# A gathered cumulative sum and projection: eight of 128 stores cut into 120 and 8 partitions

## The chip, the core and the metric

The kernel runs on one core of a Trainium2 chip. The metric is the device time of one launch, in microseconds; lower is better. Times before are the median of three runs. A profile of one execution is read beside them; its engines are PE (TensorE matmul), PEld (TensorE weight load), DVE (VectorE), ACT (ScalarE), POOL (GpSimd) and SP (SyncE).

## The reference

```python
B, S, N, D = (16, 4096, 2048, 512)
x        # (B, S, D) float32
indices  # (B, N) int64: for each batch, N different rows of S, sorted
w        # (D, D) float32

b_idx = np.arange(B)[:, None]
gathered = x[b_idx, indices, :].copy()
cs = np.cumsum(gathered, axis=1)
return np.matmul(cs, w).astype(np.float32)
```

For each of 16 batches, 2048 rows of 512 numbers are gathered, summed cumulatively along the rows, and multiplied by a 512 x 512 matrix. 67 MB are gathered and 67 MB stored.

## The kernel before

The 16 x 2048 rows are cut into T = 256 tiles of 128 rows, NT = 16 to a batch. Two tiles (R = 2) make a pair; G = 128 pairs. Each engine runs its own list of instructions, written out by hand at build time, and waits on semaphores; nothing is scheduled by a planner. `Lane.need` emits a wait only where that engine has not waited for as much before.

For each tile t the steps are:

- `gather(t)` (line 126, GpSimd): an indirect DMA brings 128 rows of x, one to a partition, into one half of a pair's buffer `g32` (8 buffers, 16 tiles). It waits until the cast of the tile 16 earlier has freed the buffer. GpSimd issues the gathers back to back, in order.
- `cast(t, n)` (line 141, ScalarE): to float16, one tile or a whole pair at once (n = 2), after the gathers of these tiles have landed. The casts run ahead of the drains by `far` tiles: 2 at the start, rising by one every 8 tiles to FAR = 10, and falling again by one every 6 tiles towards the end.
- `sums(t)` (line 152, TensorE): four matmuls against a triangular matrix give the cumulative sums within the tile, transposed. `carry(t)` (lines 171 and 184, VectorE) adds the last column of the tile before and writes float16 into `cst`.
- `project(u)` (line 195, TensorE): four matmuls by w into a PSUM bank `pb` (4 of them). TensorE's order interleaves sums and projections, with the sums up to LEAD = 4 tiles ahead, fewer at both ends.
- `drain(u)` (line 207, ScalarE): copies the PSUM bank into one half of the pair's output buffer `ob` (NO = 8 buffers of 128 partitions x 2 x 512 float32).
- `store(g)` (lines 216 and 221, SyncE): when both halves are drained, one DMA of 512 KB writes the pair, each partition holding two neighbouring rows of the output, 4 KB in a run. The triangular matrix `ut` of all pairs but the first and last puts the rows in this order. The first and last pair (`PLAIN`) keep the rows in order and are stored tile by tile.

ScalarE's list is, for each tile u: at the first tile of a pair, a wait until the store that last used this `ob` buffer has landed (the store of eight pairs earlier); then the casts due at u; then the drain of u.

```python
    for u in range(T):
        if u % R == 0:
            if u == R * NO:
                act.need(s_of, 16)
            act.need(s_o[u // R % NO], 16 * (u // R // NO))
        for t, n in casts[u]:
            cast(t, n)
        drain(u)
```

SyncE's list holds the loads of indices and w, then the 128 stores in order, then waits for the last stores to land. Every DMA adds 16 to its semaphore when all of it has landed.

Of the kernel before, what the change touches and what calls it, by code (L numbers as in the profile page):

```python
# [7 lines left out]
P = 128  # L8
# [19 lines left out]
def kernel(  # L28
# [7 lines left out]
    nc = tc.nc  # L36
# [3 lines left out]
    R = 2  # L40
# [4 lines left out]
    G = T // R  # L45
# [8 lines left out]
    NB = 4  # L54
    NC = 4
    NO = 8
    assert D == 512 and N % (R * P) == 0 and T % P == 0

    x_flat = x.rearrange("b s d -> (b s) d")
# [17 lines left out]
    cst = [const.tile([P, DC, R, P], FP16, name=f"cst{i}") for i in range(NC)]  # L77
    ob = [const.tile([P, R, D], FP32, name=f"ob{i}") for i in range(NO)]
    pa = [ps.tile([P, DC, R, Q], FP32, name=f"pa{i}") for i in range(NA)]
# [4 lines left out]
    def sem(name):  # L84
        return tc.alloc_semaphore(name)
# [9 lines left out]
    s_g = [sem(f"s_g{i}") for i in range(NG)]  # L95
    s_o = [sem(f"s_o{i}") for i in range(NO)]
    s_a = sem("s_a")
    s_d = sem("s_d")
    s_b = sem("s_b")
    s_e = sem("s_e")  # L100

    pool, pe, dve, act, sp = (
        Lane(e) for e in (nc.gpsimd, nc.tensor, nc.vector, nc.scalar, nc.sync)
    )
# [32 lines left out]
    def cast(t, n):  # L137
        g, r = divmod(t, R)
        for u in range(t, t + n):
            act.need(s_g[u % NG], 16 * (u // NG + 1))  # L140
        nc.scalar.copy(  # L141
            out=g16[g % NH][:, r : r + n], in_=g32[g % (NG // R)][:, r : r + n]
        ).then_inc(s_c, 1)
# [60 lines left out]
    def drain(u):  # L204
        g, j = divmod(u, R)
        act.need(s_b, u + 1)
        nc.scalar.copy(out=ob[g % NO][:, j], in_=pb[u % NB][:]).then_inc(s_e, 1)  # L207

    def store(g):
        b, h = divmod(g, GB)  # L210
        rows = out[b, h * R * P : (h + 1) * R * P, :]
        if g in PLAIN:
            for j in range(R):
                sp.need(s_e, R * g + j + 1)
                done = s_ol[j] if g else (s_o[0], s_of)[j]
                nc.sync.dma_start(
                    out=rows[j * P : (j + 1) * P, :], in_=ob[g % NO][:, j]
                ).then_inc(done, 16)
            return
        sp.need(s_e, R * (g + 1))  # L220
        nc.sync.dma_start(
            out=rows.rearrange("(p j) d -> p j d", j=R), in_=ob[g % NO][:]
        ).then_inc(s_o[g % NO], 16)


    with nc.allow_non_contiguous_dma(reason="a few indices, one per partition"):
        for k, eng in enumerate((nc.sync, nc.scalar)):
            t = k * R
            eng.dma_start(  # L229
                out=idx_first[:, t : t + R, :],  # L230
                in_=indices[0, t * P : (t + R) * P]
# [7 lines left out]
    for k in range(KI):  # L239
        nc.sync.dma_start(  # L240
            out=idx64[:, k, :], in_=idx_rows[k * P : (k + 1) * P, :]
        ).then_inc(s_idx[k], 16)
    for g in range(G):
        store(g)
    for g in range(G - NO, G - 1):
        sp.need(s_o[g % NO], 16 * (g // NO + 1))
    for j in range(R):
        sp.need(s_ol[j], 16)

# [5 lines left out]
        out=ident[:],  # L255
        in_=ident[:],
# [7 lines left out]
        out=ut[:],  # L264
        in_=ut[:],
# [9 lines left out]
        out=uq[:],  # L275
        in_=uq[:],
# [23 lines left out]
    for k in range(KI):  # L300
# [3 lines left out]
            out=pb[k % NB][:, :P], in_=idxf[:, k, :], identity=ident[:]  # L304
# [37 lines left out]
    for u in range(T):  # L342
        if u % R == 0:
            if u == R * NO:
                act.need(s_of, 16)
            act.need(s_o[u // R % NO], 16 * (u // R // NO))
        for t, n in casts[u]:
            cast(t, n)
        drain(u)
# [30 lines left out]
```

## Time and profile before

| | |
|---|---|
| Median of three runs (lowest, highest) | 351.18 us (350.65, 351.27) |
| The profiled execution: its own time | 351.18 us |
| Its span, first to last instruction | 349.5 us |
| Mean granted TensorE clock | 0.995 |
| PE busy, share of the span | 307.3 us, 88% |
| ACT busy | 264.2 us, 76% |
| POOL busy | 243.9 us, 70% |
| DVE busy | 179.0 us, 51% |
| Moved by DMA | 135.91 MB, mean 389 GB/s |
| Stores of a pair (line 221), median to landing | 126, 512.0 KB each, 7.4 us |
| Gathers (line 126), median to landing | 252, 8.4 us |

Busy time is summed over all stages of the run; it does not say which engine others wait for. The profiled time of 351.18 us is 1.7 us over the span: launch and end lie around it. In the list of DMA issues the last column is the median time from issue to landing. Instruction groups show count, busy time, mean duration in ns, and the idle time of the engine just before them with what ended most of it.

### The profile page before, as it was taken

The numbers are of one execution on the slowest core, as the hardware profiler recorded it, in microseconds if no ns is written. First come the engines' busy times: TensorE is split into PE (matmuls) and PEld (weight loads), VectorE is DVE, ScalarE is ACT, GpSimd is POOL, SyncE is SP. The second block draws the span as 40 slices with busy tenths as digits, with TensorE's granted clock in tenths as the row PEclk, the third lists the DMA queues.
The fourth block names the chain that finished last, engine by engine and source line by source line (L and its number), as shares of the span: only waits on it lengthen the run. The fifth ranks groups of instructions, "written<-read, shape, count | busy, mean of one in ns | idle before, by whom it ended". The sixth has DMA issues, their size and how long they took to land.

```text
span 349.5 us, 5668 instructions
## 1 busy us (share of the span) xinstructions
PE 307.3 (88%) x2071; PEld 153.9 (44%) x2071; DVE 179.0 (51%) x263; ACT 264.2 (76%) x408; POOL 243.9 (70%) x266
## 2 busy tenths in 40 slices
PE   5878877998898899999898989999898989988984
PEld 2334433554444444444444444444444445544431
DVE  1335554665554555555555545555554556654441
ACT  3368876886787778787787867777787788787883
POOL 6777777777777777777777777777777777777000
PEclk9899999999999999999999999999999999999999
DMA  7799999999999999999999999999999999999974
GB/s 238 218 299 366 389 397 399 400 399 399 403 413 409 412 409 412 415 414 413 413 416 416 409 414 412 411 411 415 410 413 412 410 415 412 414 415 415 416 320 186
DMA packets 40635, 135.91 MB, mean 389 GB/s; under 512 B 6816, under 2 KB 7072, under 8 KB 40608
## 3 DMA queue, kind: packets, MB, share of 16 engines
q0 software_dynamic: 20480, 67.13, 49.7%
q1 hardware_dynamic: 19568, 67.91, 48.3%
q10 hardware_dynamic: 560, 0.53, 0.4%
q8 instruction: 16, 0.26, 0.3%
q14 instruction: 11, 0.09, 0.1%
HBM read 68.42 MB, written 67.11 MB: 388 GB/s over the span
## 4 chain that ended last, share of the span: by engine, by line
POOL 34%; DMA 25%; issue 14%; PE 13%; ACT 11%; DVE 1%; SPq 0%; ACTq 0%
POOL g L126 34%; DMA g<-in_x_dram,idxg 24%; PE pb L195 8%; ACT g L141 8%; ACT ob L207 3%; PE pa L152 3%; DMA idx<-in_indices_dram 1%; PE pb L291 1%; DVE cst L184 1%; SPq L238 0%; DVE cst L171 0%; PE pb L303 0%; SPq L229 0%; ACTq L23 0%; DVE idxf L298 0%
## 5 line engine op out<-in xcount | busy, mean ns | idle before, releaser
L126 POOL DMA_INDIRECT g<-in_x_dram,idxg x252 | 238.4, 946 | 76.8 <-issue 67.9
L195 PE MATMUL pb<-w,cst 128*128 128x512 f16 x1024 | 262.5, 379 | 3.8 <-DVE cst L184 3.1
L184 DVE TENSOR_TENSOR cst<-pa,cst 128x512 f16<-128x512 f32 x240 | 166.0, 692 | 143.4 <-PE pa L152 143.2
L141 ACT CAST g<-g 128x1024 f16<-128x1024 f32 (+1 forms) x148 | 137.6, 931 | 54.9 <-DMA g<-in_x_dram,idxg 51.4
L207 ACT COPY ob<-pb 128x512 f32<-128x512 f32 x256 | 140.0, 586 | 23.5 <-PE pb L195 23.5
L152 PE MATMUL pa<-ut,g 128*128 128x128 f16 x1008 | 110.9, 220 | 30.3 <-ACT ob L207 19.1
L152 PEld LDWEIGHTS pa<-ut,g 128*128 128x128 f16 x1008 | 71.0, 98 | 114.3 <-ACT ob L207 45.4
L195 PEld LDWEIGHTS pb<-w,cst 128*128 128x128 f16 x1024 | 89.2, 98 | 66.5 <-DVE cst L184 3.8
L171 DVE CAST cst<-pa 128x512 f16<-128x512 f32 x16 | 11.1, 692 | 14.5 <-PE pa L152 14.5
L291 PE MATMUL pb<-zeros 128*128 128x512 f16 x21 | 8.3, 576 | 1.5 <-DVE zeros L295 1.5
L291 PEld LDWEIGHTS pb<-zeros 128*128 128x128 f16 x21 | 2.8, 137 | 5.8 <-issue 3.9
L126 POOL DMA_INDIRECT g<-in_x_dram,idx_first x4 | 4.0, 1004 | 1.6 <-issue 0.9
L298 DVE CAST idxf<-idx 128x128 f32<-128x128 uint32 x2 | 0.5, 226 | 5.8 <-DMA idx<-in_indices_dram 5.7
L338 ACT ACT_TABLE_LOAD x1 | 1.3, 1283 | 2.5 <-issue 2.5
L303 PE MATMUL pb<-ident,idxf 128*128 128x128 f32 x2 | 0.6, 315 | 2.1 <-DVE idxf L298 2.1
L341 ACT CAST w<-w 128x512 f16<-128x512 f32 x2 | 1.1, 614 | 0.6 <-DMA w<-in_w_dram 0.6
L303 PEld LDWEIGHTS pb<-ident,idxf 128*128 128x128 f32 x2 | 0.3, 139 | 3.0 <-issue 2.9
L152 PEld LDWEIGHTS pa<-uq,g 128*128 128x128 f16 x16 | 1.1, 98 | 1.2 <-ACT g L141 0.6
L152 PE MATMUL pa<-uq,g 128*128 128x128 f16 x16 | 1.4, 220 | 0.1
L295 DVE MEMSET zeros<- 128x256 uint32 x1 | 0.3, 272 | 1.1 <-SPq L82 1.1
L312 DVE CAST w<-w 128x512 f16<-128x512 f32 x2 | 0.8, 419 | 0.0
L309 DVE CAST idxg<-pb 128x128 uint32<-128x128 f32 x2 | 0.6, 292 | 0.1
(11 smaller groups left out, 2.1 us busy)
## 6 DMA issues: line engine op xcount, KB each, us to landing
out_dram<-ob SPq DMA_DIRECT2D x126, 512.0 KB, 7.4
g<-in_x_dram,idxg POOLq DMA_INDIRECT x252, 8.4
out_dram<-ob SPq DMA_DIRECT2D x4, 256.0 KB, 2.9
w<-in_w_dram ACTq DMA_DIRECT2D x2, 256.0 KB, 4.1
w<-in_w_dram SPq DMA_DIRECT2D x2, 256.0 KB, 3.5
idx<-in_indices_dram SPq DMA_DIRECT2D x2, 128.0 KB, 4.5
g<-in_x_dram,idx_first POOLq DMA_INDIRECT x4, 4.1
idx_first<-in_indices_dram ACTq DMA_DIRECT2D x1, 2.0 KB, 2.1
```

Of the source, the lines that this page charges most:

```text
L126: nc.gpsimd.indirect_dma_start(out=g32[g % (NG // R)][:, r, :], out_offset=None, in_=x_flat, in_offset=bass.IndirectOffsetOnAxis(ap=ap, ax ...
L141: nc.scalar.copy(out=g16[g % NH][:, r : r + n], in_=g32[g % (NG // R)][:, r : r + n]).then_inc(s_c, 1)
L152: mm = nc.tensor.matmul(out=pa[t % NA][:, c], lhsT=g16[g % NH][:, r, c * P : (c + 1) * P], rhs=uq[:] if g in PLAIN else ut[:], start=(c == 0),
L171: nc.vector.tensor_copy(out=dst, in_=src).then_inc(s_d, 1)
L184: nc.vector.tensor_tensor(out=dst, in0=src, in1=last, op=mybir.AluOpType.add).then_inc(s_d, 1)
L195: mm = nc.tensor.matmul(out=pb[u % NB][:], lhsT=cst[g % NC][:, c, j, :], rhs=w16[:, c, :], start=(c == 0), stop=(c == DC - 1),)
L207: nc.scalar.copy(out=ob[g % NO][:, j], in_=pb[u % NB][:]).then_inc(s_e, 1)
L291: nc.tensor.matmul(out=pb[NB - 1][:], lhsT=zeros[:, :P], rhs=zeros[:], start=True, stop=True)
L303: nc.tensor.transpose(out=pb[k % NB][:, :P], in_=idxf[:, k, :], identity=ident[:]).then_inc(s_pt, 1)
L312: nc.vector.tensor_copy(out=w16[:, c, :], in_=w32[:, c, :]).then_inc(s_wc, 1)
L338: nc.scalar.copy(out=spare[:], in_=zeros[:, :1])
L341: nc.scalar.copy(out=w16[:, c, :], in_=w32[:, c, :]).then_inc(s_wc, 1)
```

## The change

Of the 126 stores of whole pairs, those of pairs 8, 24, 40, 56, 72, 88, 104 and 120 are issued as two DMAs: partitions 0 to 119 of the buffer (480 KB), then partitions 120 to 127 (32 KB). The first adds to the buffer's own semaphore as before; the second adds to a new semaphore s_h. ScalarE waits for s_h, besides the buffer's semaphore, before it fills that buffer again (pairs 16, 32, ... 112), and SyncE waits for all eight parts at the end. Nothing else is changed: on TensorE, VectorE and GpSimd the instructions and their order are the same, and ScalarE has the same instructions with these seven waits more.

```diff
+    CUT = 120
+    SPLIT = 16
...
+    s_h = sem("s_h")
...
         sp.need(s_e, R * (g + 1))
-        nc.sync.dma_start(
-            out=rows.rearrange("(p j) d -> p j d", j=R), in_=ob[g % NO][:]
-        ).then_inc(s_o[g % NO], 16)
+        rows = rows.rearrange("(p j) d -> p j d", j=R)
+        cut = CUT if g % SPLIT == SPLIT // 2 else P
+        nc.sync.dma_start(out=rows[:cut], in_=ob[g % NO][:cut]).then_inc(s_o[g % NO], 16)
+        if cut < P:
+            nc.sync.dma_start(out=rows[cut:], in_=ob[g % NO][cut:]).then_inc(s_h, 16)
...
     for g in range(G - NO, G - 1):
         sp.need(s_o[g % NO], 16 * (g // NO + 1))
+    sp.need(s_h, 16 * (G // SPLIT))
...
             if u == R * NO:
                 act.need(s_of, 16)
+            if (u // R - NO) % SPLIT == SPLIT // 2:
+                act.need(s_h, 16 * ((u // R - NO) // SPLIT + 1))
             act.need(s_o[u // R % NO], 16 * (u // R // NO))
```

## The prediction

> **What bounds the kernel now.** I read the page first, then the list of waits, then the DMA issues window by window, then the end of the timeline.
>
> ```profile
> span 349.5 us, 5668 instructions
> ...
> POOL g L126 34%; DMA g<-in_x_dram,idxg 24%; PE pb L195 8%; ACT g L141 8%; ACT ob L207 3%; PE pa L152 3%; DMA idx<-in_indices_dram 1%; PE pb L291 1%; DVE cst L184 1%; SPq L238 0%; DVE cst L171 0%; PE pb L303 0%; SPq L229 0%; ACTq L23 0%; DVE idxf L298 0%
> ...
> L126 POOL DMA_INDIRECT g<-in_x_dram,idxg x252 | 238.4, 946 | 76.8 <-issue 67.9
> ```
>
> The chain is GpSimd's issue of gathers, and then the flight of gathers. Each gather takes 946 ns plus 0.3 us of issue: the 256 start between 3.2 and 322.4 us, one every 1.252 us, and almost nothing holds them up. So gathers are asked for at a fixed pace, and what can vary is how long after the request the rows are there.
>
> ```profile
> ACT g L141 <- DMA g<-in_x_dram,idxg: 51.4, 87, 1.3
> ```
>
> In the list of waits, ScalarE's casts wait 87 times for a gather that has not landed. The store's issuer, SyncE, waits for drains; no engine but SyncE at the very end waits for a store. Now the DMA issues of three windows (140 to 180, 220 to 260 and 300 to 324 us), with the median time from issue to landing last:
>
> ```profile
> out_dram<-ob SPq DMA_DIRECT2D x15, 512.0 KB, 7.5
> g<-in_x_dram,idxg POOLq DMA_INDIRECT x33, 8.2
> ...
> out_dram<-ob SPq DMA_DIRECT2D x15, 512.0 KB, 7.5
> g<-in_x_dram,idxg POOLq DMA_INDIRECT x33, 11.1
> ...
> out_dram<-ob SPq DMA_DIRECT2D x10, 512.0 KB, 9.8
> g<-in_x_dram,idxg POOLq DMA_INDIRECT x19, 15.1
> ```
>
> Gathers land ever later, stores hardly. A landing counts when the last of 16 parts is in: the trace keeps 16 completion events for each transfer. For the gathers issued at 140 to 180 us the last three of the 16 come on average 7.73, 7.92 and 8.15 us after the issue; at 220 to 260 us 7.99, 8.24 and 11.12; at 260 to 300 us 8.40, 9.36 and 12.63. So fifteen parts stay together and one falls behind. One DMA engine of the 16 has more to do than it can do. The page shows what such an engine could carry besides:
>
> ```profile
> q0 software_dynamic: 20480, 67.13, 49.7%
> q1 hardware_dynamic: 19568, 67.91, 48.3%
> q10 hardware_dynamic: 560, 0.53, 0.4%
> q8 instruction: 16, 0.26, 0.3%
> ```
>
> Queues 0 (gathers) and 1 (stores) fill 98% of 16 engines' span. Queue 8 moves 16 packets of instructions: 0.3% of 16 x 349.5 us is 16.8 us, about 1.05 us a packet. On one engine that is 4.8% more than the others have, which fits one straggler; that it is on one engine is inferred.
>
> Last, the timeline of ScalarE near the end:
>
> ```profile
> 314.02 1.04 ACT L141 CAST g<-g 128x1024 f16<-128x1024 f32 x1 [0.69 <-DMA g<-in_x_dram,idxg]
> ...
> 345.17 0.59 ACT L207 COPY ob<-pb 128x512 f32<-128x512 f32 x1 [0.39 <-PE pb L195]
> ```
>
> This is the last cast that waits for a gather (issued at 299.88, landed 14.04 us later). From there TensorE and ScalarE wait only for each other, for 349.46 - 314.02 = 35.4 us, in an order that the change leaves alone. So the end moves with the landing of the gather issued at 299.88. The profiled execution took 351.18 us, 1.7 over its span, and is the median of the runs shown; the sum is made against 351.18.
>
> **The change, part by part.** Eight stores (pairs 8, 24, ... 120) go as rows 0 to 119 and rows 120 to 127 of the SBUF tile. No computing instruction is added, removed or moved.
>
> *SyncE.* Eight more issues at 332 ns (the store's row), 2.7 us in all. SyncE waits 283.2 us for drains, so each delays the following store by at most 0.33 us, and no engine waits for a store: cost nothing. If stores were waited for, it would cost up to 2.7 us. The added wait at the end is for pair 120's part, issued at about 316 us and in long before the last store (landed 347.8).
>
> *ScalarE.* Before the cast that precedes the reuse of a split buffer, a wait on s_h; queued behind it are the casts, drains and, through them, TensorE's next sums. It names a transfer issued eight stores, 20 us, earlier; stores land within 11.1 us. It is met when it is reached; the semaphore instruction itself is 17 to 38 ns (line 23's row), seven times, at most 0.3 us, in time that ScalarE spends waiting. Cost nothing; if the 8-row part took over 20 us, each would stop ScalarE for the excess.
>
> *The DMA engines.* A 128-row store is 128 packets of 4 KB in 16 parts, eight rows to an engine. A packet took 159 ns (the median of the trace's packet records; page: 49.7% of 16 x 349.5 us over 16384 gather packets, less the small ones, is 167). Dealt in the same way, 120 rows fill fifteen engines and leave one out; that engine saves 8 x 159 = 1.27 us a split, and each of eight others gets one packet, 0.16 us. No row of this trace shows a 120-row transfer, so this is bounded: at one end the late engine is the one left out (-1.27 us a split); at the other the rows go fifteen to each of eight engines, the late one among them: 7 + 1 packets more, +1.27 us. I take the first end: the dealing of eight to an engine is what the 128-row stores show, and with it exactly one engine is relieved.
> The Trainium skill, "DMA: Bandwidth & Descriptors", section "Why a DMA increments its semaphore by 16 and not by 1", has a transfer on the largest number of engines up to 16 that divides its rows, the lowest-numbered first, so 120 rows would leave out engine 15 alone; its section "Latency and other measured facts" calls engines 7 and 15 usually slower. By these the gain below would stand if the late engine is 15, and turn into about +0.16 us a split if it is 7.
>
> *What the relief is worth.* Splits come every 16 stores, 16 x 2.504 = 40 us: 1.27/40 = 0.032 us per us. Landing grew from 8.2 us (window around 160) to 14.04 at 299.88: 5.84 us in 140, 0.042 per us. Left: 0.010 per us, 1.4 us, so 9.6 us in place of 14.04: a gain of 4.4. Relief before 160 us is not counted, since there the last part was already with the others. A floor: the 15th part lands at 10.0 on average for issues between 296 and 304, so while that stays the gain is at most 4.0. Something is given back: in 140 to 260 us stores moved 8.1 MB for every 8.36 of gathers, 97%, because drains were held up by late gathers. When gathers stop falling back, stores run at their pace, 3% more: 3% of 128 packets x 159 ns is 0.6 us per 40, over 140 us up to 2.1 us on every engine; nothing if they have that slack. I take a third of it, 0.7, because fourteen engines hold their landing times nearly still. 4.0 - 0.7 = 3.3: 351.2 - 3.3 = **347.9 us**. Ends of this case: 4.0 - 2.1 = 1.9 (349.3), and all lateness over the 8.2 of the early window gone, 14.04 - 8.2 = 5.8 (345.4).
> The tail takes the shift: the last gather, issued at 322.37 and landing about 10 us later, is in at 332.4, and its cast moves from 342.16 only to about 338.9.
> A rule speaks against the change: the same page, "Rules for kernel authors", says not to split a transfer by partitions, since the halves share the engines and serialize, and its "Anatomy" section puts about 2.0 us on every transfer (for the software path). By that, as an estimate, eight more would be up to 16 us if they stood on the path; the waits above show no engine waiting for a store, so the trace gives them nothing.
>
> **The rivals.**
> *The late engine takes one of the eight single rows (slower).* Then it is not relieved and gets 0.16 us at each split; in a saturated queue this adds up from about 60 us on, six splits by 300 us: +1.0 us, 352.2. For it: nothing in the records numbers the engines, and eight of 16 get a row. Against it: only that the late one may be among the other eight. It decides as soon as the late engine is not the one left out and is among those eight. With the fifteen-row dealing it would be four splits from 160 us on, +5.1, 356.3.
> *The late engine is one of the seven that neither gain nor lose.* Then its queue is as before: 351.2, within 0.2%. The same comes out if lateness is not load but a slower path of that engine to its rows, which eight packets in 256 hardly alter.
> *Another engine becomes late.* The 14th and 15th parts also rose, to 8.98 and 10.02; if these engines then grow with the faster stores, the gain is what lies between, about 1 to 1.5 us: 350.0. I count it as the slow end of faster.
>
> **How the numbers follow.** The forecast's mechanism, with its own range of 345.4 to 349.3: 0.52. Another engine late, 350.0: 0.11. No change, 351.2: 0.17. Slower, 352.2 or more: 0.20. So faster by over 0.2% (0.7 us, about what a measurement of this kernel can tell from none) 0.63, within it 0.17, slower 0.20. The range runs from 345.4 to 352.3: it takes in the milder slower case and leaves out the fifteen-row dealing and a gain over 5.8, together under 0.2.
>
> **What would show it.** Right: in the window 260 to 300 us the gathers' median landing is near 9 us in place of 12.4 and the last of the 16 parts is with the others; ScalarE's waits for gathers shrink below 51.4 us; the last cast that waits comes about 3 us earlier, and 35 us of tail follow; GpSimd's last gather still starts at 322.4. Wrong: landing still grows to 14 us (the late engine is not relieved), grows faster (it is loaded), or landing improves and the end does not move (then TensorE's 1.1 us a tile or the waits on s_h have become the bound).

## The result, and the profile after

| | before | after |
|---|---|---|
| Median (lowest to highest), four runs each | 351.23 us (350.65 to 351.38) | 352.57 us (352.15 to 352.7) |
| Ratio, 95% interval | | 1.0039 (1.0022 to 1.0057) |
| The profiled execution, its span | 351.18 us, 349.5 us | 352.7 us, 350.8 us |
| Mean granted TensorE clock | 0.995 | 0.993 |

The kernel became slower by 1.3 us (0.8 to 2.0 by the interval), where 3.3 us less was forecast. Of some kernels below a few executions took clearly longer than the others; where a number rests on such a one, it is said. The page of the changed kernel:

```profile
span 350.8 us, 5683 instructions
...
q0 software_dynamic: 20480, 67.13, 49.5%
q1 hardware_dynamic: 19624, 67.91, 48.2%
...
L129 POOL DMA_INDIRECT g<-in_x_dram,idxg x252 | 238.4, 946 | 76.8 <-issue 70.1
```

GpSimd's gathers have the same number, the same 946 ns and the same 76.8 us of idle time: requests go out at the pace of before. Queue 1 (stores) has 56 packets more for the same 67.91 MB. These are completions, 7 for each of the eight cut stores: 15 + 8 in place of 16. So the 120 rows ended in 15 parts and the 8 rows in 8, as the prediction had it.

The list of waits of the changed kernel (engine, line, what it waited for: microseconds in total, times, longest), then SyncE's:

```profile
ACT g L144 <- DMA g<-in_x_dram,idxg: 53.2, 92, 1.3
...
SPq L226 <- ACT ob L210: 281.0, 126, 4.3
```

ScalarE waits 1.8 us longer for gathers, 92 times in place of 87. No wait on s_h is in either list. SyncE's wait for drains is 2.2 us shorter (283.2 before), close to the 2.7 us that eight more issues take: the added issues lie in time in which it waited anyway.

The DMA issues of the changed kernel (count, KB each, median from issue to landing), at 140 to 180, 260 to 300 and 300 to 324 us:

```profile
out_dram<-ob SPq DMA_DIRECT2D x15, 512.0 KB, 7.1
g<-in_x_dram,idxg POOLq DMA_INDIRECT x33, 8.8
...
out_dram<-ob SPq DMA_DIRECT2D x16, 512.0 KB, 7.3
g<-in_x_dram,idxg POOLq DMA_INDIRECT x33, 13.9
out_dram<-ob SPq DMA_DIRECT2D x1, 480.0 KB, 7.5
out_dram<-ob SPq DMA_DIRECT2D x1, 32.0 KB
...
out_dram<-ob SPq DMA_DIRECT2D x10, 512.0 KB, 9.2
g<-in_x_dram,idxg POOLq DMA_INDIRECT x19, 16.4
```

Before, the same windows gave 8.2, 12.4 and 15.1 us for gathers; the middle one, which the experiments below are held against, reads:

```profile
out_dram<-ob SPq DMA_DIRECT2D x17, 512.0 KB, 7.7
g<-in_x_dram,idxg POOLq DMA_INDIRECT x33, 12.4
```

The gathers fall back faster. For gathers issued at 260 to 300 us the last three of the 16 parts came on average 8.40, 9.36 and 12.63 us after the issue; now it is 8.29, 9.36 and 14.10, so of the latest parts only the very last one changed. The records don't number the engines. If the last part belongs to the same engine in both, the late engine was not relieved but loaded further. For another engine to have taken its place, one that was at 9.36 us or earlier would have had to fall back by 4.7 us. Six cuts of the 8-row part between 60 and 300 us bring an engine 1.0 us, and the additional packets over 200 ns (see below) are worth 3.1 us in that stretch, all engines together: 4.1 us even if one engine had all of it, which falls short.

The end of ScalarE's timeline, with the last cast that waits for a gather:

```profile
312.60 1.04 ACT L144 CAST g<-g 128x1024 f16<-128x1024 f32 x1 [0.23 <-DMA g<-in_x_dram,idxg]
...
315.33 1.04 ACT L144 CAST g<-g 128x1024 f16<-128x1024 f32 x1 [0.72 <-DMA g<-in_x_dram,idxg]
```

Before, this cast started at 314.02 us. It is now 1.31 us later, and from it to the end of the span are 35.5 us (before 35.4). Its gather was issued at 299.84 us and took 15.40 us (before: at 299.88, 14.04). The whole loss lies there, in the landing of a gather.

### The profile page after: what moved, and what is told of

It reads as the page before. It is cut to its first block, busy times and chain, and to the rows that moved or that the text cites. A ratio compares the mean times of both kernels' runs of the same rounds, so it can differ in the third digit from the quotient of the medians.

```text
span 350.8 us, 5683 instructions
## 1 busy us (share of the span) xinstructions
PE 306.8 (87%) x2071; PEld 153.8 (44%) x2071; DVE 179.0 (51%) x263; ACT 264.5 (75%) x408; POOL 243.9 (70%) x266
## 3 DMA queue, kind: packets, MB, share of 16 engines
q1 hardware_dynamic: 19624, 67.91, 48.2%
## 4 chain that ended last, share of the span: by engine, by line
POOL 39%; DMA 20%; issue 15%; PE 13%; ACT 10%; DVE 1%; SPq 0%; ACTq 0%
POOL g L129 39%; DMA g<-in_x_dram,idxg 19%; PE pb L198 8%; ACT g L144 7%; ACT ob L210 3%; PE pa L155 3%; DMA idx<-in_indices_dram 1%; PE pb L297 1%; DVE cst L187 1%; SPq L243 0%; DVE cst L174 0%; PE pb L309 0%; SPq L234 0%; ACTq L23 0%; DVE idxf L304 0%
## 5 line engine op out<-in xcount | busy, mean ns | idle before, releaser
L129 POOL DMA_INDIRECT g<-in_x_dram,idxg x252 | 238.4, 946 | 76.8 <-issue 70.1
```

The source lines that it names most:

```text
L129: nc.gpsimd.indirect_dma_start(out=g32[g % (NG // R)][:, r, :], out_offset=None, in_=x_flat, in_offset=bass.IndirectOffsetOnAxis(ap=ap, ax ...
```

## The experiments

Two theories were held against each other. **F**: the late engine is one of the eight that get a row of the 8-row part, so each cut adds one packet to it. **D**: a store dealt over 15 engines has longer packets, whichever engine gets what. The two don't exclude each other, and both differ from the prediction's step, that the 15-engine store relieves the late engine. The first seven experiments cut every fourth store (32 of them) for a larger effect. Their edit to the kernel before, with only the tuple of sizes changing:

```diff
+    def parts(g):
+        return (112, 16) if g % 4 == 2 else (P,)
...
+        a = 0
+        for n in parts(g):
+            nc.sync.dma_start(out=rows[a : a + n], in_=ob[g % NO][a : a + n]).then_inc(
+                s_o[g % NO], 16
+            )
+            a += n
```

ScalarE's and SyncE's waits count the parts. All parts of a store add to the buffer's own semaphore.

### How the rows are dealt: 112 + 16, 120 + 8, 120 + 4 + 4, 120 + 7 + 1

> Every fourth store (pairs 2, 6, ... 126) goes as 112 and 16 partitions: both numbers divide by 16, so each of the 16 DMA engines still gets eight rows of it; there are 32 cuts in place of the change's 8. Theory A (the late engine is one of the eight that get a single row more): nothing is shifted between engines, so 351.2 within 0.5 and the gathers' landing in the window 260 to 300 us stays near 12.4. Rival B (the cut itself costs: another issue, another completion, another part to wait for): four times the change's +1.3, so about 356.6, with the landing near 18.

> The change's cut, 120 and 8, at every fourth store in place of every sixteenth: 32 cuts. Theory A: one packet of 0.16 us more on the late engine every 10 us; four times the change's +1.3: 356.6 (354.5 to 357), the last of the 16 parts of a gather later still, the others unmoved. Rival B: the same 356.6; it differs from A in the run with 112 and 16. Rival C (the change's +1.3 is something at single places, as the wait on its own semaphore, which this kernel has not): below 353.

> Every fourth store as 120, 4 and 4 partitions: if a transfer of n rows with n at most 15 goes to the n lowest engines, engines 0 to 3 get two rows more a cut, engines 4 to 7 none. Theory A: with the late engine among 0 to 3, +10.7, so about 362; with the late engine among 4 to 7, 351.2 within 0.7. Rival B: two more issues a cut, +10.7, 362, which the next run separates from A.

> Every fourth store as 120, 7 and 1 partitions: engines 1 to 6 get one row more a cut, engine 0 two, engine 7 none. Theory A with the late engine 7: 351.2 within 0.7 while the run with 120 and 8 is slow; with the late engine among 1 to 6: 356.6; with engine 0: 362. Rival B: 362, as with 120, 4 and 4.

| 32 cuts of | median | ratio (interval) |
|---|---|---|
| 112 + 16 | 353.04 us | 1.0051 (1.0024 to 1.0078) |
| 120 + 8 | 359.36 us | 1.0238 (1.0140 to 1.0336) |
| 120 + 4 + 4 | 359.76 us | 1.0249 (1.0097 to 1.0401) |
| 120 + 7 + 1 | 360.04 and 366.12 us, two executions | no interval |

The kernel before took 350.97 us beside them; differences in microseconds are worked out from the ratios, here and below. The 112 + 16 cut keeps the number of rows of every engine at eight (seven and one), adds an end packet of 9 ns to each, and costs 1.8 us all the same: its rows themselves must have taken longer. The three cuts with 120 rows are alike within their wide intervals (two executions each). D alone would give that. F alone would not: by the expectations, giving the single rows to four, seven or eight engines should load the late engine differently.

Where the time is can be seen in the trace's packet records, near the end of the run, where gathers are over and the store of pair 126 has the engines to itself (cut in these kernels, whole in the one before):

```
4 KB packets of the store of pair 126: mean, median, longest (ns)
kernel before, 128 rows   164  161  182
112 + 16                  212  159  614
120 + 8                   220  159  519
120 rows only             244  163  622
```

The median is the same; some packets are up to nearly four times as long. (The row of 120 rows only is from the longest of its executions, see below.) Over the whole run 0.27% of the store's 4 KB packets take over 200 ns in the kernel before, 1.02% with 32 cuts of 112 + 16 and 3.16% with 32 of 120 + 8. In the changed kernel, with eight cuts, it is 0.52%: 84 packets in place of 43, which is 7.1 us more, summed over all engines, than so many packets of 159 ns would take. One execution each: three other kernels below, whose stores are whole, have 24, 47 and (its 63 loads counted in) 76. The 41 lie mostly outside the stretch in which the gathers fall back: 56 against 26 up to 140 us, 15 against 13 from 140 to 300, 13 against 4 after that. So long packets are a property of such stores, but at the change's own eight cuts they are not seen where the time is lost.

### One part alone: 120 rows only, 112 + 8 only, and 112 + 8 + 8

The first writes partitions 0 to 119 of every fourth store, the second 0 to 119 in two parts; the third writes all.

```diff
-        return (112, 16) if g % 4 == 2 else (P,)
+        return (120,) if g % 4 == 2 else (P,)
```

> Every fourth store writes partitions 0 to 119 alone; rows of partitions 120 to 127 are left out of the output (32 x 16 rows). So one engine has eight packets less each time and no engine has more. Theory A (the late engine is charged by the 8-row part): 351 within 1, landing in the window 260 to 300 us near 12.4. Theory D (a store dealt over 15 engines is itself slower, whatever becomes of the eight rows): near the 359 of 120 and 8. If the late engine is the fifteenth's left-out neighbour after all: below 348, landing near 9.

> Every fourth store as 112 partitions (seven rows to each of 16 engines) and 8; the last eight partitions are left out of the output. Eight engines keep eight rows, eight others have one row less every 10 us, 0.16 us, 0.016 us per us. Theory A (late engine among the eight that get the small part): as the run with 112 and 16, 353 within 1. If the late engine is among the other eight: the growth of landing of 0.042 falls to 0.026, 2.2 us less by 300 us, about 351. Theory D: no store over 15 engines here, so 353 or below.

> Every fourth store as 112, 8 and 8 partitions, all rows stored: eight engines get nine rows, eight others seven, and no transfer runs over 15 engines. Theory A: one packet more on the late engine as with 120 and 8: 357 to 359. Theory D: near the 353 of 112 and 16. If the late engine is among the eight that get seven: about 351.

Beside 351.26 us of the kernel before: 120 rows only took 355.75 us, ratio 1.0104 (1.0065 to 1.0143); 112 + 8 only 353.32 us, 1.0070 (1.0046 to 1.0094). The four executions of 112 + 8 + 8 are far apart, 356.50, 360.77, 362.09 and 363.26 us; the ratio on record, 1.0305, lies above the two lower ones (1.015 and 1.027). DMA issues of the kernel with 120 rows only at 260 to 300 us, two of its waits, and a piece of its chain near the end:

```profile
out_dram<-ob SPq DMA_DIRECT2D x12, 512.0 KB, 9.9
out_dram<-ob SPq DMA_DIRECT2D x4, 480.0 KB, 9.1
g<-in_x_dram,idxg POOLq DMA_INDIRECT x33, 17.1
...
ACT ob L215 <- DMA out_dram<-ob: 2.4, 3, 1.6
ACT g L149 <- DMA out_dram<-ob: 1.4, 1, 1.4
...
314.97 17.52 DMA out_dram<-ob
```

This is the prediction's gain tried by itself: one engine has eight packets less at each of 32 stores, no engine has one more, a sixteenth of the bytes of these stores is gone, and the time rises by 3.7 us. By the step of the prediction it should have fallen to 347.9 us or below. The trace is of the longest of the five executions, 361.82 us (the others took 354.13 to 356.52). In it gathers land at 17.1 us in place of 12.4, and stores land so late, one after 17.52 us, that ScalarE waits for them, which it does neither in the kernel before nor in the changed one; the last cast that waits for a gather starts at 318.56 us, 4.5 later than before, and the rest of that execution's loss lies behind it. So the relief is not to be had, and the store over 15 engines costs something of its own: 3.7 us for 32, or 0.9 for eight if it is proportional. In the cut 112 + 8 only, no engine has more than its eight rows (seven and one), and the time still rises by 2.5 us. There the gathers' last part comes at 14.63 us (before 12.63) while the second latest comes earlier, 7.53 (before 9.36). D holds, and not for 15 engines alone: 112 rows run over 16.

112 + 8 + 8 puts two single rows on the same eight engines, nine in all; in 112 + 16 each of the 16 has eight. The traced executions took 356.50 and 353.00 us: 3.5 us more. The last cast that waits for a gather starts at 318.36 us in place of 315.54, and the last part comes at 17.25 us in place of 14.22. Packets over 200 ns from 140 to 300 us are alike, 33 and 30. That is F's direction and near its size: 24 cuts between 60 and 300 us at 0.16 us are 3.8 (32 transfers more by themselves would be some 0.3 us, by the 63 loads below). So the late engine is most likely among the eight. I have no account for the three longer executions of 112 + 8 + 8.

### Single rows without any cut

Every store goes whole; besides, small loads go out on the same queue into a buffer that nothing reads. The first kernel issues 63 loads of one row, the second eight loads of eight rows after the very stores that the change cuts.

```diff
+        if g % 16 == 8:
+            k = g // 16 * 8
+            nc.sync.dma_start(
+                out=extra[k : k + 8], in_=x_flat.rearrange("(p j) d -> p (j d)", j=R)[k : k + 8]
+            ).then_inc(s_x, 16)
```

> The same kernel as e12: no store is cut, 63 single rows of 4 KB are loaded through the store's queue. Here a run of the kernel before takes 351. Theory F (the late engine is the one to which every single-row transfer falls): 10 us more on it, landing in the window 260 to 300 us above 16, time 357 to 361. If the late engine is another: 351.2 within 0.7.

> The same kernel as e13: eight loads of eight rows, no store cut. Theory F: +0.7 to +1.2, so 352.2; theory D: 351.2 within 0.4.

The kernel before took 351.46 us beside them. 63 one-row loads: 352.04 us, ratio 1.0014 (1.0005 to 1.0024). Eight loads of eight rows: 352.28 us, 1.0026 (1.0014 to 1.0038). DMA issues at 260 to 300 us and the last cast that waits for a gather, of the one and then of the other:

```profile
g<-in_x_dram,idxg POOLq DMA_INDIRECT x33, 12.2
extra<-in_x_dram SPq DMA_DIRECT2D x8, 4.0 KB
...
314.08 1.05 ACT L143 CAST g<-g 128x1024 f16<-128x1024 f32 x1 [0.54 <-DMA g<-in_x_dram,idxg]
```

```profile
g<-in_x_dram,idxg POOLq DMA_INDIRECT x33, 13.1
extra<-in_x_dram SPq DMA_DIRECT2D x1, 32.0 KB
...
315.02 1.04 ACT L143 CAST g<-g 128x1024 f16<-128x1024 f32 x1 [0.76 <-DMA g<-in_x_dram,idxg]
```

Eight loads, 64 rows in all, are enough to bring the gathers' landing from 12.4 to 13.1 us and that cast from 314.02 to 315.02 us: +1.0 us there and +0.9 in the time. It is the price that the prediction's first rival worked out (six splits by 300 us, 0.16 us each). The long packets do not come with it: 47 over 200 ns, before 43. This is F's part of the loss, taken without D's. How large it is, is less sure: the 63 one-row loads move nearly as many bytes, leave the cast at 314.08 us and still cost 0.5 us (0.2 to 0.8), and the interval of the eight loads (0.5 to 1.3) overlaps with that. Four times 0.9 for 32 cuts and the 3.7 of 120 rows only make 7.3 us; the 120 + 8 cut cost 8.4 (4.9 to 11.8), so the two parts together can account for it.

63 loads of one row have one completion each, so one engine takes each of them. If it is always the same one, it has 63 x 0.16 = 10 us more to carry, and the late part doesn't care: 12.2 us. The second latest rises instead, from 9.36 to 10.76 us on average (and the third latest from 8.40 to 9.88, which one engine's load doesn't explain). So, if it is always the same one, that engine is not the late one, but had room for most of the 10 us. That every one-row transfer goes to the same engine is what the page states that the prediction cites ("DMA: Bandwidth & Descriptors", "Why a DMA increments its semaphore by 16 and not by 1"); no run here numbers the engines.

### Less code to fetch

Each output tile is summed over two of the four blocks of w: half of the projection is left out, and a quarter of TensorE's instructions.

```diff
-        for c in range(DC):
-            if c == 2 and t is not None:
+        for c in (0, DC - 1):
+            if c == DC - 1 and t is not None:
```

> Stores as before; the projection uses two of its four chunks of w (the products of the middle half of the columns are left out), so TensorE has 1024 instructions less of 4142 and a quarter less to fetch: 12 packets of 16 KB in place of 16, 4.2 us less. If the late engine is late because it fetches TensorE's instructions: queue 8 shows 12 packets and the landing in the window 260 to 300 us falls from 12.4 to 8 to 10 us, the last of the 16 parts with the others; the time falls by that and by the shorter tail, to 338 to 346. If fetching is not its cause: landing 12 or more there; the time falls by the tail alone.

Measured: 349.19 us beside 351.26, ratio 0.9939 (0.9920 to 0.9957). From the page, then the DMA issues at 260 to 300 us and ScalarE's last two casts that wait for a gather:

```profile
q8 instruction: 12, 0.20, 0.2%
```

```profile
g<-in_x_dram,idxg POOLq DMA_INDIRECT x32, 12.7
...
314.20 1.04 ACT L141 CAST g<-g 128x1024 f16<-128x1024 f32 x1 [0.68 <-DMA g<-in_x_dram,idxg]
...
333.25 0.62 ACT L141 CAST g<-g 128x512 f16<-128x512 f32 x1 [0.40 <-DMA g<-in_x_dram,idxg]
```

Four of the 16 packets of instructions are gone, 4.2 of the 16.8 us that the prediction suspected on the late engine. If they had made it late, the growth between 160 and 300 us (0.042 us per us) would have been less by 4.2/350 = 0.012, and the landing better by some 1.7 us. It is 12.7 us, and the last part comes at 12.86 us, where it was at 12.63: no relief is to be seen. With half of the projection left out, the tail is no longer TensorE's and ScalarE's alone: the last cast that waits for a gather is now the one at 333.25 us, whose gather was issued at 317.56 and took 15.62 us, so the late part still sets the end. This trace is of the longest of the four executions, 350.31 us; the others took 349.11 to 349.25, and where they gained their 1.1 us no trace shows. So the run speaks against the fetch as the cause and doesn't exclude it. Why one engine is late stays open.

### What told nothing

In two groups of runs the kernel before itself took 451.41 and 444.82 us, at clocks near 0.89, and more than half of the completion records are missing from the traces; there a difference of 1 us is not to be seen, and the late part cannot be followed.

```diff
+            nc.sync.dma_start(out=rows[:, j : j + n], in_=ob[g % NO][:, j : j + n]).then_inc(
...
+        for _ in range(16):
+            nc.sync.sem_inc(s_x, 1)
```

Cut by columns (the first line, 128 partitions of 2 KB twice at every fourth store):

> Every fourth store as two transfers of all 128 partitions, each one output row of 2 KB to a partition: a cut that leaves the dealing of partitions to engines as it is. Cost to every engine: 16 packets of 84 ns in place of 8 of 159, +0.07 us, and one completion more, 32 times: up to +2.6, spread over all engines alike. Theory D (the dealing makes packets long): no long packets; in the quiet stretch at the end those of pair 126 take 84 to 90 ns; 351.2 to 353. Rival B (any cut makes them long): long packets there as with 112 and 16 (mean 212 against 164 ns of 4 KB), 353 or more.

The eight stores of the change with 120 rows only, tried twice:

> The change's eight cut stores without their 8-row parts: partitions 120 to 127 of these pairs are left out of the output. No engine has a packet more than before, one has eight less at each cut. Theory D (packets of a store dealt over 15 engines are longer): a quarter of the +3.6 that 32 such stores cost, +0.9, so 352.1. Theory F (the cost is the single row on the late engine, which is the first of the engines): 351.2 within 0.4.

> The eight stores of the change write partitions 0 to 119 only; the rows of the other 8 partitions are left out. Theory D (a store over 15 engines has longer packets and loads the late engine with them): a quarter of the +3.6 to +4.5 us that 32 such stores cost, so +0.4 to +1.1 us, 351.6 to 352.3, last part at 260 to 300 us near 13.2. Rival (the whole loss of the change is the eight single rows): 351.2 within 0.2 us, last part 12.6. The prediction's step (late engine left out): 347.9, last part near 9.

The loads of one and of eight rows, which were then repeated with the results above:

> No store is cut. After every second store one row of 4 KB is loaded from x into one partition of a scratch tile, through the same queue: 63 transfers of a single packet, which, as the single row of 120, 7 and 1 did, should all fall to one and the same engine. Theory F (that engine is the late one): 0.16 us every 5 us more on it, 10 us in all: landing in the window 260 to 300 us above 16, time 357 to 361. If the late engine is another: the loaded engine has as much more as the late one had (16.8 us by queue 8) or less, so 351.2 within 0.7.

> No store is cut. Besides, after each of the eight stores that the change cuts, one load of eight rows of 4 KB (from x into a scratch tile, one row to each of eight partitions) goes through the same queue: the 8-row part's burden without the cut. Theory F: the late engine gets 0.16 us more at each of them, 1.3 in all, of which the part before 60 us is absorbed: +0.7 to +1.2, 352.2. Theory D: nothing, 351.2 within 0.4.

32 loads of eight and of seven rows, to tell which of the eight engines is late, and 2016 increments more on SyncE (the last line of the diff):

> No store is cut; after every 4th pair store (32 times) a load of 8 rows x 4 KB goes out on the same queue, into a buffer that nothing reads. One row on each of eight engines, so 32 x 0.16 = 5.1 us more for each of them. Theory F (the late engine is one of the eight that take the rows of an 8-row transfer): four times the eight loads' +0.9 us, so +3.6 to +5 us (354.9 to 356.3), gathers issued at 260 to 300 us land after about 16 us in place of 12.4. Rival (the lateness comes from something else that the eight loads did, the late engine is not among them): 351.2 to 352, landing 12.4.

> As with loads of 8 rows, but 7 rows each: one row on each of seven engines, the eighth gets nothing. If the late engine is the eighth of them: 351.2 to 352, landing at 260 to 300 us as before, 12.4 us. If it is among the second to the seventh: as the 8-row loads, +3.6 to +5 us (354.9 to 356.3), landing about 16 us. If the late engine is none of the eight, both runs stay near 351.5.

> 16 more semaphore increments on SyncE after each pair store, 2016 instructions, which change nothing else; their code has to be fetched. If the fetch of instructions of an engine lies on the late DMA engine, its load grows by some 16 packets of 0.3 us, about 5 us over the run: the gathers issued at 260 to 300 us land about 3 us later and the time is 354 to 356. If it does not: 351.2, landing 12.4.

| | ratio (interval) |
|---|---|
| cut by columns, 32 times | 0.9979 (0.9935 to 1.0022) |
| 120 rows only, 8 times | 0.9954 (0.9897 to 1.0010); 1.0047 (1.0003 to 1.0090) |
| 63 loads of one row | 1.0054 (1.0013 to 1.0095) |
| 8 loads of eight rows | 0.9960 (0.9914 to 1.0007) |
| 32 loads of eight rows | 1.0024 (0.9946 to 1.0101) |
| 32 loads of seven rows | 1.0067 (1.0027 to 1.0107) |
| SyncE's increments | 1.0440 (1.0346 to 1.0533) |

No verdict is taken from these, with one exception: near the end of the kernel whose stores are cut by columns, the 512 packets of 2 KB of pair 126 and of the last pair take 86.8 ns on average, the longest 107; in the kernel before, the last pair's 256 take 86.1, the longest 100. There, cutting a store in two did not lengthen packets, each half having all 128 partitions. The increments were badly chosen besides: SyncE's wait for drains fell from 283.2 to 41.4 us, so they filled its time and held stores up, whatever their code cost to fetch.

## Why the prediction was wrong, step by step

*The chain, and what sets the end: held.* GpSimd's pace (its last gather starts at 322.3 us, before 322.4), the tail of 35.4 us and the place to look were right. (In the tail TensorE also waits once for VectorE, 1.0 us, which the prediction's "only for each other" leaves out.) The end moved with the landing of the gathers: the cast that waits +1.31 us, the median +1.34.

*SyncE and ScalarE at nothing: held.* SyncE's eight issues came out of its waiting, and no wait for s_h is in the lists.

*How the rows are dealt: held as far as the records go.* Each cut store has 15 + 8 completions.

*Which end was taken for it: this step failed.* The prediction took "-1.27 us a split", since 120 rows relieve exactly one engine and exactly one is late. Nothing in the profile tied these two engines together, and the prediction said so in its own rival ("nothing in the records numbers the engines"). By count alone one engine of 16 is left out, eight get a row more, seven neither, and still the one had more than half of the chance. In the changed kernel the last part came at 14.10 us in place of 12.63, where near 9 was forecast, and with 120 rows only, 32 times, the time rose by 3.7 us: the engine left out is not the late one. The rival's term, +0.16 us a cut on the late engine, fits: it gave +1.0 us, 352.2, and 352.57 was measured; eight loads of eight rows by themselves cost +0.9 us (0.5 to 1.3).

*The packet's price: too small for stores that don't span 128 partitions.* All terms used 159 ns for a packet of any store. That is the 128-row store's; a store of 120 or 112 rows has some packets of 500 to 600 ns. What is left of 1.34 after the 0.9 is 0.4 us, and 32 stores of 120 rows would give 3.7/4 = 0.9 for eight if it is proportional. But from 140 to 300 us the changed kernel has hardly more long packets than before (15 and 13), and the runs with eight stores of 120 rows could not tell. So whether D has a part in the change's own loss is not shown.

*The inferred cause of the lateness: not borne out.* With a quarter less fetching of TensorE's instructions the landing was 12.7 us in the one execution traced. This did not enter the sum, but it made a lateness by load look certain.

*The rates of relief and the give-back of 0.7 us* were never put to the test, since there was no relief.

*The rules of the Trainium skill.* "DMA: Bandwidth & Descriptors", section "Latency and other measured facts", calls engines 7 and 15 usually slower. With rows dealt to the lowest-numbered engines, engine 7 is the last of the eight that get a row, and engine 15 the one left out. The runs bear out neither. Engine 15 is excluded above. For engine 7, the cuts into 120 + 4 + 4 and 120 + 7 + 1 should then cost only what 120 rows alone cost, 3.7 us (2.3 to 5.0), since by that dealing engine 7 gets none of the single rows; their four executions lay 6.5 to 15.2 us above the kernel before. That speaks against engine 7, as far as F and D simply add up. The loads of seven rows would have told more. The rule against splitting by partitions (same page, "Rules for kernel authors") had the sign right. The fixed cost of a transfer that would have gone with it was not seen: 63 transfers more cost 0.5 us.

**Open:** why one engine is late, which one, where the long packets of a store over fewer than 128 partitions come from, and what part they have in the change's own loss.

## What to carry to other kernels

When one of 16 DMA engines sets the end, an edit to how rows are dealt is worth what it does to that engine; as long as the records don't say which engine it is, count how many places relieve it and how many load it, and let the chances follow the count. A cheap test is to leave out the doubtful half or to add it alone: 120 rows without the other eight, or eight rows without the cut. In these traces a store that spans all 128 partitions kept its packets short, and one row more on each of eight engines, eight times, already cost about a microsecond on a saturated queue.

## What the runs showed of the hardware

- A store of 120 or of 112 partitions has packets of up to 519 to 622 ns where nothing else runs; the 128-partition store's longest there is 182 ns. When a store is cut by columns, no 2 KB packet near the end is over 107 ns.
- Eight loads of eight 4 KB rows, some 1.3 us in all on each of eight engines, move the end by 0.9 us (0.5 to 1.3), while 63 loads of one row, with one completion each, move it by 0.5 (0.2 to 0.8) and the last cast that waits for a gather by 0.06: where the same bytes go makes the difference at that cast, in one execution each.
- With a 16th of the bytes left out at every fourth store (120 partitions of 128), the kernel became slower, by 3.7 us (2.3 to 5.0).
